# A decoder block on one core: weight buffers moved within 512 bytes, and a few aligned matmuls put ahead of others

## The chip, the cores and the metric

The kernel runs on 1 core of one Trainium2 chip. The metric is device time in microseconds (us), the median of several runs; less is better. TensorE (PE in the profile) does the matmuls, and its weight loads stand under PEld. VectorE is DVE, ScalarE is ACT, GpSimd is POOL; SP issues most DMAs.

## The reference

One decoder layer on 256 tokens of width 1024, float32:

```python
h = rms_norm(x, norm_mix_g);  x = x + hybrid_mixer(h, ...)      # gated convolution and sparse attention, one output projection
h = rms_norm(x, norm_x_g);    x = x + cross_attention(h, mem)   # 4 heads of 256 over 256 memory tokens
h = rms_norm(x, norm_ffn_g);  x = x + swiglu(h, w_in, w_out)    # 1024 -> 2 x 2816 -> 1024
return rms_norm(x, final_norm_g)
```

In `hybrid_mixer` one large projection of `h` gives the convolution's input and gate, 16 queries of 64, three pairs of keys and values (compressed, selected, window; 4 groups) and three sets of gates. With 256 tokens every block of 64 is selected and the window covers everything, so the selected and the window branch are two full causal attentions with their own keys and values.

## The kernel before

**How a float32 product is made.** Activations lie transposed, features on partitions, in eight blocks of 128 features by 256 tokens. A weight chunk is 1024 x 256 and is loaded in two halves of four 128-row blocks (`raw`, L236). `split` (L172) makes a high half (ScalarE copies it rounded to fp32r, L184) and a low half (VectorE subtracts, L186). An activation is parted the same way (`part`, L323). A product is then weight high by activation high, weight high by activation low, weight low by activation high: `rows` (L269, matmuls at L280), 8 matmuls for each of the three in a half, so 48 for a chunk. A matmul has a stationary operand (`lhsT`, 128 x 128, loaded ahead by a weight load) and a moving one (`rhs`, 256 or 512 columns). In most chunks the weight is stationary and the activation moves; with `nat=True` (vs, vw, v) the activation is stationary and the weight moves. A few products (`whole`, L301: k0, kc, vc, q) run in plain fp32 without a split.

**Order of the work.** Memory keys k0 to k3; the convolution's input u0 to u7; kc, vc and queries; ks, kw, vs, vw (keys and values of both branches); gates ga and gc and memory values v, in between which the eight pairs of heads go through `scores`, `weights`, `turned` (transposes, L816) and `output` (L822); pw (convolution's output projection), wo, cross-attention (xq, `cross_scores`, `cross_output`, xo), feed-forward f0 to f21 (L1101), its output fo (L1141), the final norm. The framework's planner orders instructions by priority, but `in_line()` and `behind()` fix the order of most matmuls. The matmuls of xq and xo are only partly fixed.

**A pair's scores** (`scores`, L749): the keys of a group are `kdh` and `kdl`, both branches side by side. For each head a query block of the later 128 tokens meets all 256 keys of both branches (512 moving columns, L761), and one of the first 128 tokens meets 128 keys of both (256 columns, L769). TensorE's order is later half of head 0, first half of heads 0 and 1, later half of head 1. VectorE adds the bias and finds the minimum, first the first halves of both heads (L774), then the later ones (L780); ScalarE takes the exponentials (L795), first halves first. The first halves' PSUM bank, tag `s0`, has one buffer, and the next `turned("b...")` takes it.

**Feed-forward** (L1101 to L1123): for each chunk the high weights meet both parts of the activation in one product of 512 columns (L1113: two outputs of 8 blocks each), then the low weights meet the high part, 256 columns (L1111, 2 x 8). The activation lies in one tile, blocks 0 to 6 as `g`, block 7 as `g8`.

**Where the operands lie.** A tile keeps its place within a partition; a pool gives its tags room in the order of first use. The long slots L0 to L6, L9, LL, L10, L14, L12, L11, L13 come first. The first starts at a multiple of 512 bytes; each is 8,192 bytes except LL (16,896 = 33 x 512) and L14 (8,448 = 16.5 x 512, for `kdl`). So L12, L11 and L13 begin 256 bytes past a multiple of 512 and the others on one. Behind them stands `gap` (L399, 80 elements, 320 bytes), so the five high buffers (`whi`) and the five low ones (`wlo`) begin at 64 modulo 512; each is 4,096 bytes, so all five do. What follows (two small tiles, `vt`, `pr`, `sg`, then `w`, which holds the feed-forward's low halves and the other chunks' raw weights) begins at 128 or, for every second `vt`, at 384. Three halves are placed apart by `set_apart` (L195): k3_0, xq1_0 and xo0_0 have their high half at 256 and their low half at 448.

Below, the **offset** of an operand is its first byte modulo 512, and the **difference** is moving offset minus stationary offset, modulo 256. All rows and blocks within a tile are multiples of 512 apart except where the columns of a block of 256 begin in its second 128, which is 512 bytes on, so a tile has one offset.

Of the kernel before, what the change touches and what calls it, by code (L numbers as in the profile page):

```python
# [10 lines left out]
F32R = mybir.dt.float32r  # L11
# [4 lines left out]
P = 128  # L16
D = 1024
S = 256
# [80 lines left out]
def tile_hybrid_block(  # L99
# [26 lines left out]
    def longs(names, slots, dt=F32R):  # L126
        return [long(n, i, dt=dt) for n, i in zip(names, slots)]
# [6 lines left out]
    def small(name, shape, dt=F32, tag=None, bufs=1):  # L134
        return sb.tile(shape, dt, tag=tag or name, name=name, bufs=bufs)
# [35 lines left out]

    def split(w, shape, name):  # L172
        if name in apart:
            hi = apart[name]()[:, 64:].rearrange("p (k c) -> p k c", k=shape[1])
        else:
            hi = small(f"{name}h", shape, F32R, tag="whi", bufs=5)
        if name in apart:
            lo = aparts[name]().rearrange("p (k c) -> p k c", k=shape[1])
        else:
            lo = small(f"{name}l", shape, F32R, **places[1 - into_ffn(name)])  # L180

        n = 2 if name == "k1_0" else shape[1]
        with behind(*first.get(name, ())):
            copies = [nc.scalar.activation(hi[:, at:at + n], w[:, at:at + n], AF.Copy) for at in range(0, shape[1], n)]  # L184
            for at in range(0, shape[1], n):
                low = nc.vector.tensor_tensor(out=lo[:, at:at + n], in0=w[:, at:at + n], in1=f(hi[:, at:at + n]), op=ALU.subtract)  # L186
        splits[name] = copies[-1], low
        return hi, lo
# [1 line left out]

    first, splits, apart = {}, {}, {}

    aparts = {}

    def set_apart(name, tag, low=None):  # L195

        pair = []

        def hi():
            pair.append(sb.tile([P, 1024 + 64 if low else 2 * 1024 + 112], F32R, tag=tag, name=f"{name}h"))  # L200
            return pair[0][:, 0:1024 + 64]

        def lo():
            if low:
                return sb.tile([P, 1024 + 112], F32R, tag=low, name=f"{name}l")[:, 112:]
            return pair[0][:, 1024 + 112:]

        apart[name], aparts[name] = hi, lo

    set_apart("k3_0", "L14", "L10")  # L210
    set_apart("xq1_0", "LL")
    set_apart("xo0_0", "LL")

# [19 lines left out]
    def into_ffn(name):  # L233
        return name[0] == "f" and name[1] != "o"
# [143 lines left out]
        nc.tensor.matmul(warm, lhsT=ones, rhs=ones, start=True, stop=True)  # L378


    memh, meml, hh, hl, kxh, kxl = longs(("memh", "meml", "hh", "hl", "kxh", "kxl"), range(6))
    mem, h = (memh, meml), (hh, hl)
    mem_t, hf = longs(("mem_t", "hf"), (6, 9), F32)
    _, xt_t, sq = twin("xtsq", F32)
    w = held["k0"] = long("k0w", 10, (P, NB, 256))
# [10 lines left out]
        ahead(name, slot)  # L396
    roots(0)

    small("gap", [P, 80])  # L399

    def kx(j):
        ps = gemm(f"k{j}", mem) if j else whole("k0", mem_t)
# [4 lines left out]
    for i in range(2):  # L407
        hs = slice(4 * i, 4 * i + 4)
        part(memh[:, hs], meml[:, hs], mem_t[:, hs])
    kx(1)  # L410
    for i in range(2):
        hs = slice(4 * i, 4 * i + 4)
        nc.scalar.activation(sq[:, hs], xt_t[:, hs], AF.Square)
# [65 lines left out]
    def convolve(n_v, n_g, *marks):  # L479
# [7 lines left out]
                next(on_g, None)  # L487
        tc.cur_priority = here

    for j in range(NB):  # L490
        ps = gemm(f"u{j}", h)
        sg = small(f"sg{j}", [P, S], tag="sg", bufs=3)
        act = nc.scalar.activation(sg, ps[:, 1], AF.Sigmoid)
        vec = nc.vector.tensor_tensor(out=vt[j][:, PAD:], in0=ps[:, 0], in1=sg, op=ALU.mult)
        convolve((0, 4, 6, 6, 8, 8, 10, 12)[j], (0, 2, 3, 3, 4, 4, 4, 4)[j], act, vec)
# [250 lines left out]
    def heads_of(hp):  # L746
        return 2 * hp, 2 * hp + 1

    def scores(hp):  # L749

        g = hp // 2
        nbp = bias_of(hp)
        s0 = aux(f"s0_{hp}", [P, 2, 2, P], "s0", 1)
        p0 = small(f"p0_{hp}", [P, 2, 2, P], tag="p0", bufs=2)
        s1s, p1 = [], []

        def later_half(hd):
            s1 = aux(f"s1_{hd}", [P, 2, S], "s", 2)
            with in_line():
                for i, t in enumerate((kdh, kdl)):  # L760
                    mm = nc.tensor.matmul(s1, lhsT=qh(hd, 1), rhs=t[:, g].rearrange("p b t -> p (b t)"), start=i == 0, stop=i == 1)  # L761
            last[:] = [mm]
            s1s.append(s1)

        later_half(2 * hp)
        for k, hd in enumerate(heads_of(hp)):
            with in_line():
                for i, t in enumerate((kdh, kdl)):
                    mm = nc.tensor.matmul(s0[:, k], lhsT=qh(hd, 0), rhs=t[:, g, :, 0:P], start=i == 0, stop=i == 1)  # L769
        last[:] = [mm]  # L770
        later_half(2 * hp + 1)
        for k, hd in enumerate(heads_of(hp)):
            for br in range(2):
                red = nc.vector.tensor_tensor_reduce(out=p0[:, k, br], in0=s0[:, k, br], in1=nbp[:, k, P:S], scale=1.0, scalar=3e38,  # L774
                                                     op0=ALU.add, op1=ALU.min, accum_out=mins[:, hd, 0, br:br + 1])
        for k, hd in enumerate(heads_of(hp)):
            p1.append(small(f"p1_{hd}", [P, 2, S], tag="pr", bufs=4))
            for br in range(2):
                with behind(red):
                    low = nc.vector.tensor_tensor_reduce(out=p1[k][:, br], in0=s1s[k][:, br], in1=nbp[:, k], scale=1.0, scalar=3e38,  # L780
                                                   op0=ALU.add, op1=ALU.min, accum_out=mins[:, hd, 1, br:br + 1])
        mins_of.append(low)
        if hp == 1:
            first["gc2_1"] = red,
        return p0, p1

    def weights(hp, p0, p1, *late):

        exp = []
        for qb in range(2):  # L790
            for k, hd in enumerate(heads_of(hp)):
                for br in range(2):
                    t = p1[k][:, br] if qb else p0[:, k, br]
                    with behind(*late) if qb else ExitStack():
                        exp.append(nc.scalar.activation(t, t, AF.Exp, scale=-1.0, bias=mins[:, hd, qb, br:br + 1],  # L795
                                                        accum_out=sums[:, hd, qb, br:br + 1]))
        sc = sums[:, 2 * hp:2 * hp + 2].rearrange("p h t b -> p (h t b)")
        nc.vector.scalar_tensor_tensor(out=sc, in0=sc, scalar=1e-30, in1=igd[:, 2 * hp:2 * hp + 2].rearrange("p h t b -> p (h t b)"),
                                       op0=ALU.max, op1=ALU.mult)
        nc.vector.reciprocal(sc, sc)  # L800
        for k, hd in enumerate(heads_of(hp)):
            for br in range(2):
                nc.vector.tensor_scalar(out=p1[k][:, br], in0=p1[k][:, br], scalar1=sums[:, hd, 1, br:br + 1],
                                        scalar2=None, op0=ALU.mult)
                norm = nc.vector.tensor_scalar(out=p0[:, k, br], in0=p0[:, k, br], scalar1=sums[:, hd, 0, br:br + 1],
                                               scalar2=None, op0=ALU.mult)
        return exp[-1], norm
# [149 lines left out]
    def residual(products, xin, gain, name, slots):  # L957

        xo = long(f"x_{name}", slots[0])
        if len(slots) == 1:  # L960
            t = sb.tile([P, 2 * NB * S + 128], F32R, tag="LL", name=f"g_{name}")
            g = t[:, 16:16 + 14 * S].rearrange("p (c k s) -> p c k s", c=2, k=NB - 1)
            g8 = t[:, 80 + 14 * S:80 + 16 * S].rearrange("p (c s) -> p c s", c=2)
            gh, gl = ([g[:, c, k] if k < NB - 1 else g8[:, c] for k in range(NB)] for c in range(2))
        else:
            gh, gl = longs((f"gh_{name}", f"gl_{name}"), slots[1:])
            xg_ = gh, gl
            gh, gl = ([t[:, k] for k in range(NB)] for t in xg_)
# [87 lines left out]
    def later_half(names, x):  # L1056
# [3 lines left out]
        for n, ps in zip(names, pss):  # L1060
# [5 lines left out]
            if n == names[2]:  # L1066
# [14 lines left out]

    rf = small("rf", [P, S], tag="vw", bufs=4)
    nc.scalar.activation(rf, spread(rnorm(acc2, "3"), "3"), AF.Copy)
    uh, ul = ([long(f"u{c}{i}", n, (P, 6 * S + 16), F32R)[:, 16:].rearrange("p (k s) -> p k s", k=6) for i, n in enumerate(ss)]
              for c, ss in (("h", (4, 2, 1, 12)), ("l", (5, 3, 6, 13))))
    def residual_first():

# [13 lines left out]
    for j in range(NF):  # L1101
        hs = chunk(f"f{j}")
        ab = small(f"ab{j}", [P, 2, S], tag="pr", bufs=4)
        pss = [bank(f"ps_f{j}_{b}") if j % 2 == 0 else aux(f"ps_f{j}_{b}", [P, 2, S], "s", 2) for b in range(2)]
        for part_ in range(2):
            for b, ps in enumerate(pss):
                cs = slice(b * P, b * P + P)
                for kb in range(NB):
                    w = hs[kb // 4][part_][:, kb % 4, cs]
                    if part_:  # L1110
                        nc.tensor.matmul(ps[:, 1], lhsT=w, rhs=fg(kb)[:, 0], start=False, stop=kb == NB - 1)  # L1111
                    else:
                        nc.tensor.matmul(ps, lhsT=w, rhs=fg(kb), start=kb == 0, stop=False)  # L1113
        for b, ps in enumerate(pss):
# [187 lines left out]
```

## Time and profile before

| | us |
|---|---|
| median of 3 runs (550.94 to 551.54) | 551.5 |
| the profiled execution | 551.26 |
| its span, first to last instruction | 549.2 |
| VectorE busy in the span | 417.9 |
| ScalarE busy | 360.4 |
| GpSimd busy | 140.0 |

The span is one execution seen by the profiler; 2.06 us of the execution's own time lie outside it. Engines' busy times overlap. In lists of instructions the form of a line is start, length, engine, source line, operation, output<-inputs, shapes and count; a length reaches from the first start to the last end, and the matmuls are pipelined, so the time of one in a row of them is the difference between starts, not its own length. Buffer numbers are left out of names, so that `k_0h` is the first high half of any of k1 to k3. Transfers bring 512 KB per half chunk, and the f chunks land 3.7 us (median) after their issue.

### The profile page before, as it was taken

What the parts mean: (1) busy time and instruction counts of PE and PEld (TensorE: products, weight loads), DVE (VectorE), ACT (ScalarE), POOL (GpSimd) and SP (SyncE); (2) the same over time, 40 slices, a digit from 0 to 9 for tenths busy, and PEclk for the clock granted to TensorE, in tenths of its full rate; (3) what the DMA queues carried; (4) which work ended last, traced back from release to release, by engine and by line L of the source; (5) the groups of instructions that cost most, each with busy time, mean ns of one, the idle gap of its engine ahead of it and who ended that gap; (6) DMA issues with size and microseconds to landing.
All of it is one profiled execution on the core that took longest, in us unless ns stands there. A gap on an engine that the chain in (4) does not pass through costs nothing.

```text
span 549.2 us, 10209 instructions
## 1 busy us (share of the span) xinstructions
PE 541.3 (99%) x3886; PEld 501.3 (91%) x3886; DVE 417.9 (76%) x781; ACT 360.4 (66%) x681; POOL 140.0 (25%) x125
## 2 busy tenths in 40 slices
PE   8999999999999999999999999999999999999995
PEld 7999998899999999889999999988888888888884
DVE  3888977999998998894868675559878787965531
ACT  4677667679956899689547674477565656463431
POOL 0005999999995001000004100310000000000001
PEclk9999999999999999999999999999999999999999
DMA  8939714456366445334556640466565555177611
GB/s 303 416 125 341 291 25 132 130 170 238 124 214 191 153 144 177 106 116 155 185 198 203 226 150 1 158 226 215 194 204 178 203 175 175 38 237 255 197 40 76
DMA packets 29297, 97.30 MB, mean 177 GB/s; under 512 B 3136, under 2 KB 5440, under 8 KB 28992
## 3 DMA queue, kind: packets, MB, share of 16 engines
q1 hardware_dynamic: 28816, 95.86, 52.3%
q10 hardware_dynamic: 432, 0.79, 0.4%
q8 instruction: 30, 0.49, 0.4%
q14 instruction: 19, 0.16, 0.1%
HBM read 95.39 MB, written 1.25 MB: 176 GB/s over the span
## 4 chain that ended last, share of the span: by engine, by line
PE 94%; DMA 2%; issue 1%; DVE 1%; ACT 1%; SPq 0%; POOLq 0%; POOL 0%; DVEq 0%
PE ps_f L1113 15%; PE fo L1141 10%; PE ps_u L280 8%; PE ps_f L1111 7%; PE ps_q L310 5%; PE ps_ga L280 4%; PE ps_v L280 4%; PE ps_gc L280 4%; PE ps_pw L280 4%; PE ps_xq L280 4%; PE ps_k L280 3%; PE ps_xo L280 3%; PE ps_wo L280 2%; PE ps_xo L1073 2%; PE s L761 1%
## 5 line engine op out<-in xcount | busy, mean ns | idle before, releaser
L466 POOL TENSOR_TENSOR yt<-yt,vw 128x512 f32<-128x512 f32 x61 | 97.0, 1592 | 51.0 <-ACT vw L464 47.4
L464 ACT ACTIVATE vw<-vt,ppt 128x256 f32<-128x256 f32 x102 | 44.3, 498 | 11.4 <-POOL yt L466 11.3
L1113 PE MATMUL ps_f<-g,f_0h 128*128 128x512 f32 x176 | 47.8, 394 | 0.1
L1113 PE MATMUL ps_f<-g,f_1h 128*128 128x512 f32 x176 | 47.6, 391 | 0.0
L1183 POOL TENSOR_SCALAR x<-x,rr 128x512 f32<-128x512 f32 x1 | 0.7, 699 | 176.4 <-DVE rr L1153 176.4
L450 DVE SCALAR_TENSOR_TENSOR yp<-vt,ppt,yp 128x256 f32<-128x256 f32 x108 | 44.1, 480 | 0.2
L186 DVE TENSOR_TENSOR f_0l<-f,f_0h 128x1024 fp32r<-128x1024 f32 x22 | 26.9, 1223 | 19.6 <-PE ps_f L1111 19.6
L1113 PEld LDWEIGHTS ps_f<-g,f_1h 128*128 128x128 f32 x176 | 32.7, 188 | 6.9
L184 ACT ACTIVATE f_1h<-f 128x1024 fp32r<-128x1024 f32 x22 | 23.3, 1060 | 23.2 <-PE ps_f L1113 20.0
L1113 PEld LDWEIGHTS ps_f<-g,f_0h 128*128 128x128 f32 x176 | 31.5, 189 | 5.6 <-DVE ab L1116 0.3
L795 ACT ACTIVATE p<-p,mins 128x128 f32<-128x128 f32 (+1 forms) x64 | 28.3, 445 | 6.7 <-DVE mins L774 6.6
L310 PE MATMUL ps_q<-hf,q 128*128 128x256 f32 x128 | 28.5, 381 | 0.0
L1111 PE MATMUL ps_f<-g,f_0l 128*128 128x256 f32 x176 | 28.1, 281 | 0.0
L1111 PE MATMUL ps_f<-g,f_1l 128*128 128x256 f32 x176 | 28.0, 281 | 0.0
L186 DVE TENSOR_TENSOR f_1l<-f,f_1h 128x1024 fp32r<-128x1024 f32 x22 | 26.8, 1218 | 0.6 <-ACT f_1h L184 0.6
L1111 PEld LDWEIGHTS ps_f<-g,f_0l 128*128 128x128 f32 x176 | 25.5, 188 | 1.8
L310 PEld LDWEIGHTS ps_q<-hf,q 128*128 128x128 f32 x128 | 24.1, 190 | 3.3
L184 ACT ACTIVATE f_0h<-f 128x1024 fp32r<-128x1024 f32 x22 | 23.0, 1046 | 1.8 <-DMA f<-in_wst_dram 1.8
L1111 PEld LDWEIGHTS ps_f<-g,f_1l 128*128 128x128 f32 x176 | 23.9, 189 | 0.0
L1115 ACT ACTIVATE ab<-ps_f 128x256 f32<-128x256 f32 x44 | 16.4, 376 | 6.8 <-PE ps_f L1111 6.8
L981 POOL COPY acc<-s_wo 128x256 f32<-128x256 f32 x1 | 1.1, 1122 | 72.1 <-ACT s_wo L974 72.1
L324 ACT ACTIVATE uh<-sl 128x256 fp32r<-128x256 f32 x22 | 9.2, 418 | 14.3 <-DVE sl L1120 14.3
(550 smaller groups left out, 1555.1 us busy)
## 6 DMA issues: line engine op xcount, KB each, us to landing
f<-in_wst_dram SPq DMA_DIRECT2D x44, 512.0 KB, 3.7
fo<-in_wfo_dram SPq DMA_DIRECT2D x20, 512.0 KB, 4.0
u<-in_wst_dram SPq DMA_DIRECT2D x14, 512.0 KB, 5.7
q<-in_wst_dram SPq DMA_DIRECT2D x8, 512.0 KB, 5.3
ga<-in_wst_dram SPq DMA_DIRECT2D x8, 512.0 KB, 3.7
gc<-in_wst_dram SPq DMA_DIRECT2D x8, 512.0 KB, 3.7
v<-in_wst_dram SPq DMA_DIRECT2D x8, 512.0 KB, 4.3
pw<-in_wst_dram SPq DMA_DIRECT2D x8, 512.0 KB, 5.0
```

Of the source, the lines that this page charges most:

```text
L184: copies = [nc.scalar.activation(hi[:, at:at + n], w[:, at:at + n], AF.Copy) for at in range(0, shape[1], n)]
L186: low = nc.vector.tensor_tensor(out=lo[:, at:at + n], in0=w[:, at:at + n], in1=f(hi[:, at:at + n]), op=ALU.subtract)
L280: mm = nc.tensor.matmul(ps[:, b], lhsT=lhsT, rhs=rhs, start=row + b + kb == 0, stop=kb == NB - 1 and row == 2 and b == 1)
L310: mm = nc.tensor.matmul(ps[:, b], lhsT=w[:, k, cs], rhs=x[:, kb], start=kb + b == 0, stop=kb == NB - 1 and b == 1)
L450: nc.vector.scalar_tensor_tensor(out=out[:, i] if t == ts[-1] else acc[i], in0=v, scalar=w, in1=acc[i], op0=ALU.mult, op1=ALU.add)
L464: nc.scalar.activation(pr[:, i], v, AF.Identity, scale=w, bias=col(PP_DB, j + i) if t == 0 else 0.0)
L466: nc.gpsimd.tensor_tensor(out=y, in0=y, in1=pr, op=ALU.add)
L795: exp.append(nc.scalar.activation(t, t, AF.Exp, scale=-1.0, bias=mins[:, hd, qb, br:br + 1], accum_out=sums[:, hd, qb, br:br + 1]))
L1111: nc.tensor.matmul(ps[:, 1], lhsT=w, rhs=fg(kb)[:, 0], start=False, stop=kb == NB - 1)
L1113: nc.tensor.matmul(ps, lhsT=w, rhs=fg(kb), start=kb == 0, stop=False)
L1115: nc.scalar.activation(ab[:, b], ps[:, 0], AF.Copy)
L1141: nc.tensor.matmul(accs[c][tb], lhsT=t, rhs=w[:, k], start=False, stop=kb == NF - 1 and t is tl)
```

## The change

No matmul, load or arithmetic is added or left out. Operands move, and some instructions change places.

- `gap` shrinks from 80 to 48 elements, so all `whi` and `wlo` buffers begin at 448 instead of 64; `vt` moves to 0 and 256, `pr` to 0; a new `gap2` of 32 elements ahead of `sg` keeps `sg` and `w` where they were.
- `set_apart` places only a high half, at the start of a long slot; the low half goes into the ordinary low ring. k3_0 (offset 0 now), xq1_0 and xo0_0 (0) stay apart, ks_0 (256, slot L11) and k1_0 (0, slot 2) are new. `hh` is allocated after k1 in slot 2.
- The parts of the cross-queries shift with `vt`, from 320 and 64 to 192 and 448.
- A pair's scores are ordered head by head, later half then first half, so that the last two products are those of 256 columns. VectorE's reductions and ScalarE's exponentials go head by head as well.
- In the feed-forward `g` moves from 64 to 192 and `g8` from 320 to 384; the low half begins with block 7 of both outputs, then blocks 0 to 6. Its result `uh`, `ul` moves by 128 bytes, as the output's weights do.

What this makes of the differences:

| products | before | after |
|---|---|---|
| weight stationary (k, u, ks, kw, ga, gc, pw, wo, xq, xo) | 192 | 64 |
| weight moving (vs, vw, v) | 64 | 192 |
| high half of k3_0, xq1_0, xo0_0 | 0 | 0 |
| high half of k1_0, ks_0 | 192 | 0 |
| low half of k3_0, xq1_0, xo0_0 | 64 | 64 |
| pairs' scores; cross outputs; fo | 0 | 0 |
| cross-scores | 192 | 64 |
| f, high weights, blocks 0 to 6 / block 7 | 0 / 0 | 0 / 192 |
| f, low weights, blocks 0 to 6 / block 7 | 192 / 192 | 64 / 0 |

```diff
     def split(w, shape, name):
         if name in apart:
-            hi = apart[name]()[:, 64:].rearrange("p (k c) -> p k c", k=shape[1])
+            hi = apart[name]().rearrange("p (k c) -> p k c", k=shape[1])
         else:
             hi = small(f"{name}h", shape, F32R, tag="whi", bufs=5)
-        if name in apart:
-            lo = aparts[name]().rearrange("p (k c) -> p k c", k=shape[1])
-        else:
-            lo = small(f"{name}l", shape, F32R, **places[1 - into_ffn(name)])
+        lo = small(f"{name}l", shape, F32R, **places[1 - into_ffn(name)])
...
+    def set_apart(name, tag):
+        apart[name] = lambda: sb.tile([P, 1024], F32R, tag=tag, name=f"{name}h")
+
+    set_apart("k3_0", "L14")
+    set_apart("ks_0", "L11")
     set_apart("xq1_0", "LL")
     set_apart("xo0_0", "LL")
...
+    early = long("k1_0h", 2, (P, 1024), F32R)
+    apart["k1_0"] = lambda: early
...
-    small("gap", [P, 80])
+    small("gap", [P, 48])
...
+    hh = long("hh", 2, dt=F32R)
+    h = hh, hl
...
+    small("gap2", [P, 32])
...
         later_half(2 * hp)
+        first_half(0)
         later_half(2 * hp + 1)
+        first_half(1)
+        low = ()
         for k, hd in enumerate(heads_of(hp)):
             p1.append(small(f"p1_{hd}", [P, 2, S], tag="pr", bufs=4))
+            for br in range(2):
+                with behind(*low):
+                    red = nc.vector.tensor_tensor_reduce(out=p0[:, k, br], in0=s0[:, k, br], in1=nbp[:, k, P:S], scale=1.0, scalar=3e38,
+                                                         op0=ALU.add, op1=ALU.min, accum_out=mins[:, hd, 0, br:br + 1])
...
-        for qb in range(2):
-            for k, hd in enumerate(heads_of(hp)):
+        for k, hd in enumerate(heads_of(hp)):
+            for qb in range(2):
...
-            g = t[:, 16:16 + 14 * S].rearrange("p (c k s) -> p c k s", c=2, k=NB - 1)
-            g8 = t[:, 80 + 14 * S:80 + 16 * S].rearrange("p (c s) -> p c s", c=2)
+            g = t[:, 48:48 + 14 * S].rearrange("p (c k s) -> p c k s", c=2, k=NB - 1)
+            g8 = t[:, 96 + 14 * S:96 + 16 * S].rearrange("p (c s) -> p c s", c=2)
...
-    uh, ul = ([long(f"u{c}{i}", n, (P, 6 * S + 16), F32R)[:, 16:].rearrange("p (k s) -> p k s", k=6) for i, n in enumerate(ss)]
+    uh, ul = ([long(f"u{c}{i}", n, (P, 6 * S + 48), F32R)[:, 48:].rearrange("p (k s) -> p k s", k=6) for i, n in enumerate(ss)]
...
-        for part_ in range(2):
+        for part_, kbs in ((0, range(NB)), (1, (NB - 1,)), (1, range(NB - 1))):
             for b, ps in enumerate(pss):
                 cs = slice(b * P, b * P + P)
-                for kb in range(NB):
+                for kb in kbs:
```

More of the change, by code (lines that the diff above doesn't have):

```diff
@@ L191, in tile_hybrid_block @@
     first, splits, apart = {}, {}, {}
[L193 to L210, printed above, removed]
+    def set_apart(name, tag):
+        apart[name] = lambda: sb.tile([P, 1024], F32R, tag=tag, name=f"{name}h")
+    set_apart("k3_0", "L14")
+    set_apart("ks_0", "L11")
     set_apart("xq1_0", "LL")
@@ L378, in tile_hybrid_block @@
         nc.tensor.matmul(warm, lhsT=ones, rhs=ones, start=True, stop=True)
-    memh, meml, hh, hl, kxh, kxl = longs(("memh", "meml", "hh", "hl", "kxh", "kxl"), range(6))
-    mem, h = (memh, meml), (hh, hl)
+    memh, meml, kxh, kxl = longs(("memh", "meml", "kxh", "kxl"), (0, 1, 4, 5))
+    mem = memh, meml
+    early = long("k1_0h", 2, (P, 1024), F32R)
+    apart["k1_0"] = lambda: early
+    hl = long("hl", 3, dt=F32R)
     mem_t, hf = longs(("mem_t", "hf"), (6, 9), F32)
@@ L763, in later_half, with first_half @@
             s1s.append(s1)
-        later_half(2 * hp)
-        for k, hd in enumerate(heads_of(hp)):
+        def first_half(k):
             with in_line():
                 for i, t in enumerate((kdh, kdl)):
-                    mm = nc.tensor.matmul(s0[:, k], lhsT=qh(hd, 0), rhs=t[:, g, :, 0:P], start=i == 0, stop=i == 1)
-        last[:] = [mm]
+                    mm = nc.tensor.matmul(s0[:, k], lhsT=qh(2 * hp + k, 0), rhs=t[:, g, :, 0:P], start=i == 0, stop=i == 1)
+            last[:] = [mm]
+        later_half(2 * hp)
+        first_half(0)
         later_half(2 * hp + 1)
[L772 to L775, printed above, removed]
+        first_half(1)
+        low = ()
         for k, hd in enumerate(heads_of(hp)):
             p1.append(small(f"p1_{hd}", [P, 2, S], tag="pr", bufs=4))
+            for br in range(2):
+                with behind(*low):
+                    red = nc.vector.tensor_tensor_reduce(out=p0[:, k, br], in0=s0[:, k, br], in1=nbp[:, k, P:S], scale=1.0, scalar=3e38,
+                                                         op0=ALU.add, op1=ALU.min, accum_out=mins[:, hd, 0, br:br + 1])
             for br in range(2):
@@ L781, in scores @@
                                                    op0=ALU.add, op1=ALU.min, accum_out=mins[:, hd, 1, br:br + 1])
-        mins_of.append(low)
+            low = low,
+        mins_of.append(low[0])
         if hp == 1:
@@ L789, in weights @@
         exp = []
-        for qb in range(2):
-            for k, hd in enumerate(heads_of(hp)):
+        for k, hd in enumerate(heads_of(hp)):
+            for qb in range(2):
                 for br in range(2):
@@ L1104, in tile_hybrid_block @@
         pss = [bank(f"ps_f{j}_{b}") if j % 2 == 0 else aux(f"ps_f{j}_{b}", [P, 2, S], "s", 2) for b in range(2)]
-        for part_ in range(2):
+        for part_, kbs in ((0, range(NB)), (1, (NB - 1,)), (1, range(NB - 1))):
             for b, ps in enumerate(pss):
                 cs = slice(b * P, b * P + P)
-                for kb in range(NB):
+                for kb in kbs:
                     w = hs[kb // 4][part_][:, kb % 4, cs]
                     if part_:
-                        nc.tensor.matmul(ps[:, 1], lhsT=w, rhs=fg(kb)[:, 0], start=False, stop=kb == NB - 1)
+                        nc.tensor.matmul(ps[:, 1], lhsT=w, rhs=fg(kb)[:, 0], start=False, stop=kb == NB - 2)
                     else:
```

## The prediction

> **What bounds the kernel now.** I read the head of the page first: the span, TensorE's busy time, its clock.
>
> ```profile
> span 549.2 us, 10209 instructions
> PE 541.3 (99%) x3886; PEld 501.3 (91%) x3886; DVE 417.9 (76%) x781; ACT 360.4 (66%) x681; POOL 140.0 (25%) x125
> PEclk9999999999999999999999999999999999999999
> ```
>
> TensorE is busy for all but 7.9 us at the full clock, so only a change in the time of its 3886 matmuls can move the end by much. The change removes and adds none. What can differ is the step, the time from one matmul's start to the next. Next came the chain in order of time (start, length, what, count); its length over its count is the step of a row without a break.
>
> ```profile
> 13.16 5.65 PE ps_k L280 x48
> ...
> 31.94 42.84 PE ps_u L280 x378
> ...
> 121.98 5.65 PE ps_ks L280 x48
> ...
> 138.95 5.65 PE ps_vw L280 x48
> ...
> 168.60 5.66 PE ps_ga L280 x48
> 174.26 5.65 PE ps_gc L280 x48
> ...
> 181.31 3.77 PE ps_gc L280 x32
> ...
> 189.61 4.72 PE ps_gc L280 x40
> ...
> 256.15 21.97 PE ps_pw L280 x192
> ...
> 344.39 8.48 PE ps_xo L1073 x72
> 352.87 5.65 PE ps_xo L280 x48
> ...
> 389.30 3.65 PE ps_f L1113 x16
> 392.95 1.89 PE ps_f L1111 x16
> ...
> 484.84 55.80 PE fo L1141 x246
> ```
>
> All L280, L1073 and L1111 rows are the same shape, 128x128 stationary and 256 moving columns. Yet 42.84/378 is 113.3 ns and 5.65/48 is 117.7 (117.8 over many). u and ks even have equal offsets (moving 0, stationary 64). So one and the same pair of offsets runs at a **short** (113.3) or a **long** (117.8) step, and keeps it over dozens of matmuls: something survives from matmul to matmul, which I call the phase. The third step is in the timeline of TensorE around the second half of k, where k3_0's high half lies at 256 and its low half at 448 (start, length, engine, line; the difference of starts over 8 is the step).
>
> ```profile
> 26.51 1.12 PE L280 MATMUL ps_k<-meml,k_0h 128*128 128x256 f32 x8
> 27.47 1.07 PE L280 MATMUL ps_k<-memh,k_0l 128*128 128x256 f32 x8
> 28.38 1.07 PE L280 MATMUL ps_k<-memh,k_1h 128*128 128x256 f32 x8
> ```
>
> At difference 0 (moving offset minus stationary, modulo 256) the step is 0.96/8 = 120 ns, the **aligned** step; the first eight at difference 64 behind it take 0.91, so 113.3. The same view, later, at the end of the cross outputs (difference 0) and the scores behind them (difference 192):
>
> ```profile
> 330.22 0.64 PE L1038 MATMUL xo_ps<-pxl,vxh 128*128 128x256 f32 x4
> 330.70 0.64 PE L1012 MATMUL xs<-kxh,xqh 128*128 128x256 f32 x4
> 331.17 0.64 PE L1012 MATMUL xs<-kxl,xqh 128*128 128x256 f32 x4
> ```
>
> 0.48/4 = 120 again, then 0.47/4 = 117.5: behind an aligned stretch, 192 goes long where 64 went short. That is the core of the forecast: an aligned stretch sets the phase, and the difference that follows picks the step.
>
> **The change part by part.** Its gain is 4.5 ns for each matmul that goes from the long to the short step, its price 2.2 ns for each long one that becomes aligned (6.7 where it was short). Everything is counted from the profiled execution: 549.2 us of span and 2.06 outside, 551.26, against a median of 551.5.
>
> *k1.* The first 16 go to offset 0, the other 32 to difference 64: 16 x 120 + 32 x 113.3 = 5.55 against 5.65, -0.11. k2's first 24 start behind a short fp32 break; 0, bounds -0.11 to +0.11.
>
> *ks, kw, vs, vw.* Four groups of 48, of which the chain shows the first and last, have the long step: 22.6 us. Afterwards ks_0's high half is aligned (16 at 120) and 176 follow at 113.3: 21.9, so -0.76. vs and vw swap operands and go from 64 to 192; k3's rows show the short step surviving such a crossing (k_0l to k_1h, 64 to 192).
>
> *Gates behind scores.* ga3 and gc0 (96), 32 of gc1 and 40 of gc2 follow a pair's scores and have the long step: 168 matmuls, 19.80 us. Now a pair ends with two aligned 256-column products and the gates stand at difference 64: 168 x 113.3 = 19.04, -0.76. The scores themselves keep their products; 0, bounds +-0.2.
>
> *v behind scores.* It goes to 192, which the cross-score rows put at the long step behind aligned work. It has that now too. 0.
>
> ```profile
> 216.15 1.10 PE L280 MATMUL ps_v<-v_1h,meml 128*128 128x256 f32 x8
> 217.09 0.40 PE L761 MATMUL s<-kdh,qt 128*128 128x512 f32 x1
> ...
> 218.51 1.10 PE L280 MATMUL ps_v<-v_1l,memh 128*128 128x256 f32 x8
> 219.45 1.10 PE L280 MATMUL ps_v<-v_0h,memh 128*128 128x256 f32 x8
> ```
>
> *Restarts.* A stretch that starts behind fp32 work falls into one step or the other. The first row here is such a stretch, at difference 64: 0.94/8, long. Starts at 192 behind the same kind of transpose are mostly short, and so is pw, 21.97/192 = 114.4 with its start. The change swaps the two differences: v's restarts (100 long matmuls) may gain 0.45, the gates' (168 short, ga0 to ga2 among them) may lose 0.76, pw and wo (336) 1.5, xq and what lies between its exchanges -0.3 to +0.7. I take 0, as it is now, since no row shows a start of 64 behind the long fp32 output that precedes pw; all ends stay in the range.
>
> *xo.* Behind the last cross output (aligned) 72 + 48 matmuls run at the long step at 192. They go to 64: 120 x 4.5 = -0.54.
>
> *Feed-forward.* A chunk in the steady part takes 3.65 + 1.89. The low half would be 2 x 120 + 14 x 113.3 = 1.83 instead of 1.89, -0.06. The high half's wide products take 228.1 each against 55.80/246 = 226.8 in the output; if they inherit the better phase, another -0.02 at most, but two of 16 now stand at 192, which no wide row shows: bounds -0.02 to +0.02. I take half, -0.075 a chunk, and 20 of 22 chunks (the first are broken up): -1.5. The output's differences stay 0.
>
> *What else moves.* The second head's two first-half reductions now stand behind the first head's two later-half ones on DVE's queue, and that bank is what the next pt_b needs.
>
> ```profile
> 211.66 0.42 DVE L780 CUSTOM_DVE_ANT_0 p<-s,nb 128x256 f32<-128x256 f32 x1
> 213.86 0.64 PE L816 MATMUL pt_b<-cpt,p 128*128 128x128 f32 x4
> ```
>
> Here first-half reductions end before 211.66, pt_b starts at 213.86, 2.2 us later; two reductions cost 0.84. Cover holds, unless a 1.2 us split gets between; without it TensorE waits a few tenths at each of seven pairs, at most 2 us. The exponentials are the same eight in another order, used a period later: 0. k1_0 and ks_0 leave the ring of five high buffers; k3_0, xq1_0 and xo0_0 bring their low halves into the ring of five low ones. No load is added or moved on SP's or POOL's queue; low halves may be written later by one buffer's turn, at most 24 matmuls or 2.7 us, and TensorE is 99% busy, so I take 0.
>
> Sum: -0.11 - 0.76 - 0.76 - 0.54 - 1.5 = -3.7; 551.26 - 3.7 = **547.6 us**.
>
> The Trainium skill speaks against all of it. Its page "SBUF — State Buffer", section "A bandwidth-pool intuition that's wrong (but worth ruling out)", gives TensorE a second, independent read port for weight loads, and "TensorE: Matmul & The Clock Gate", section "Back-to-back issue gap", makes the step depend on the columns alone (109 ns for 256, by its formula). By these the sum is 0. The trace disagrees: 113.3, 117.7 and 120 for one shape at the full clock.
>
> **The rivals.** *Offsets are not the cause* (the change doesn't do what it says): then the phase comes with what runs around the matmuls and the time stays 551.3. For it: u and ks share their offsets. Against it: all aligned stretches quoted step 120, and no other does. This is the rival that the two rules above give. *Two are too few*: k3's and the cross outputs' aligned stretches are 16 and 24 long, the feed-forward's and the scores' only 2, behind wide ones. Then -1.5 and -0.76 go: 549.8. *Restarts turn*: pw and wo start long, +1.5, a little more from xq: 549.2. *On the other side*: difference 64 does not hold the short step. Quoted rows show it for 8 matmuls, and v has the long one there. Its place is the u loop: if its 378 fall to 117.8 within a chunk, so do k3, ga, pw, wo, xq, some 1000 short ones now, +4.5, while the five gains are gone: about 555.8. Even with the five gains kept it ends slower once some 820 of them turn (820 x 4.5 = 3.7). Better than the forecast by more than a microsecond: v's restarts gain, wides too.
>
> **How the numbers follow.** Forecast with its bounds (546.0 to 548.6) 0.49; two too few 0.16; restarts turn 0.15; offsets not the cause 0.10; other side 0.07; better still 0.03. The range takes the first three and leaves out 0.20: 546.0 to 550.5. About 0.2%, 1.1 us, is what a measurement here tells from no change: faster (under 550.4) 0.80, the first three and the last less 0.03 for the far end of the second; within 0.2% 0.13, that and the offsets' case; slower 0.07.
>
> **What would show it.** In the changed trace, by the differences of starts: k1's first 16 at 120 and the rest at 113.3; ks likewise, and kw, vs, vw 5.44 each; gc behind scores 113.3; u still 42.8 for 378; pw and wo as now; L1073 8.16 for 72; a chunk's L1111 group 1.83 and its L1113 group 3.63 to 3.65. An L1111 group still at 1.89 makes the second rival right, a pw of 22.6 the third, a u of 44.5 the fourth. A wait of TensorE on DVE or ACT at pt_b, or on a split at L186, would break the assumption that nothing else counts. The forecast is wrong altogether if the steps are not set where operands lie.

## The result, and the profile after

The changed kernel takes **555.88 us** (median of 4 runs, 555.58 to 556.23) against 551.22 for the kernel before in the same session: a ratio of 1.0086, 95% interval 1.0069 to 1.0104. It is slower by 4.7 us; 547.6 was forecast. The profiled execution took 556.06, its span is 554.0 against 549.2.

From the head of the page:

```profile
span 554.0 us, 10209 instructions
PE 544.4 (98%) x3886; PEld 503.2 (91%) x3886; DVE 418.9 (76%) x781; ACT 360.0 (65%) x681; POOL 139.9 (25%) x125
```

TensorE is busy 3.1 us longer with the same 3886 matmuls, and idle 9.6 us instead of 7.9. The chain in order of time (start, length, what, count) shows where; L264 is L280 of before, L1068 L1073, L1108 L1113, L1106 L1111.

```profile
13.09 5.54 PE ps_k L264 x48
...
32.02 44.52 PE ps_u L264 x378
...
123.75 5.53 PE ps_ks L264 x48
129.28 5.44 PE ps_kw L264 x48
134.72 5.66 PE ps_vs L264 x48
...
170.45 5.65 PE ps_ga L264 x48
...
258.60 21.96 PE ps_pw L264 x192
...
348.70 6.02 PE ps_xo L1068 x53
...
437.97 3.70 PE ps_f L1108 x16
441.67 1.89 PE ps_f L1106 x16
```

k1, ks and kw came as forecast, to 0.02 us (5.54, 5.53 and 5.44 for 48), and L1068 runs at 6.02/53 = 113.6. But u, which the forecast left at 42.84, takes 44.52, vs kept its long step, the gates behind scores (ga3 here) too, and a feed-forward chunk takes 3.70 + 1.89 instead of 3.65 + 1.89. The steps of each group, added up in the two traces:

| group | forecast, us | measured, us |
|---|---|---|
| k1, k2, k3 | -0.11 | +0.13 |
| u | 0 | +1.70 |
| ks, kw, vs, vw | -0.76 | -0.34 |
| gates behind scores | -0.76 | 0 |
| gates at restarts (ga0 to ga2, the ends of gc1 and gc2, gc3) | 0 | +0.6 |
| v, its wait at pt_b left out | 0 | -0.5 |
| wait at pt_b | 0 | +0.9 |
| wo3 and xq, 0.4 of it waits | 0 | +1.0 |
| xo, all 192 products | -0.54 | -0.44 |
| feed-forward, wide and narrow | -1.5 | +0.5 |
| x's transposes into fo and fo itself, with the wait ahead of f0's last products | 0 | +1.3 |

The table adds up to 4.9; the difference of the spans is 4.8. The last row is mostly one wait, in TensorE's timeline:

```profile
369.31 1.66 PE L1108 MATMUL ps_f<-g,f_1h 128*128 128x512 f32 x6 [0.93 <-DVE g L973]
```

The -0.54 for xo was meant for the 72 products of L1068 and the 48 behind them; these gained 0.53, and the products of xo ahead of them lost 0.09.

### The profile page after: what moved, and what is told of

It reads as the page before. It is cut to its first block, busy times and chain, and to the rows that moved or that the text cites. A ratio compares the mean times of both kernels' runs of the same rounds, so it can differ in the third digit from the quotient of the medians.

```text
span 554.0 us, 10209 instructions
## 1 busy us (share of the span) xinstructions
PE 544.4 (98%) x3886; PEld 503.2 (91%) x3886; DVE 418.9 (76%) x781; ACT 360.0 (65%) x681; POOL 139.9 (25%) x125
## 4 chain that ended last, share of the span: by engine, by line
PE 93%; DMA 2%; DVE 2%; issue 1%; ACT 1%; SPq 0%; POOLq 0%; POOL 0%; ACTq 0%; DVEq 0%
PE ps_f L1108 14%; PE fo L1136 10%; PE ps_u L264 8%; PE ps_f L1106 8%; PE ps_q L294 5%; PE ps_ga L264 4%; PE ps_gc L264 4%; PE ps_xq L264 4%; PE ps_pw L264 4%; PE ps_v L264 3%; PE ps_wo L264 3%; PE ps_k L264 3%; PE ps_xo L264 2%; PE pt_a L811 1%; PE ps_kc L294 1%; PE o L835 1%
## 5 line engine op out<-in xcount | busy, mean ns | idle before, releaser
L455 POOL TENSOR_TENSOR yt<-yt,vw 128x512 f32<-128x512 f32 x61 | 94.4, 1549 | 53.6 <-DMA vcw<-in_wst_dram 46.2
L1108 PE MATMUL ps_f<-g,f_1h 128*128 128x512 f32 x176 | 48.1, 394 | 0.9 <-DVE g L973 0.9
L1108 PE MATMUL ps_f<-g,f_0h 128*128 128x512 f32 x176 | 48.1, 395 | 0.0
L1108 PEld LDWEIGHTS ps_f<-g,f_1h 128*128 128x128 f32 x176 | 32.7, 188 | 8.4 <-DVE g L973 1.2
L1108 PEld LDWEIGHTS ps_f<-g,f_0h 128*128 128x128 f32 x176 | 31.4, 188 | 5.9
L1106 PE MATMUL ps_f<-g,f_1l 128*128 128x256 f32 x176 | 31.6, 280 | 0.0
L1106 PEld LDWEIGHTS ps_f<-g,f_1l 128*128 128x128 f32 x176 | 26.9, 188 | 1.8
L1106 PE MATMUL ps_f<-g,f_0l 128*128 128x256 f32 x176 | 28.4, 281 | 0.0
L1106 PEld LDWEIGHTS ps_f<-g,f_0l 128*128 128x128 f32 x176 | 24.1, 188 | 0.1
```

The lines of the kernel that those rows point to most:

```text
L455: nc.gpsimd.tensor_tensor(out=y, in0=y, in1=pr, op=ALU.add)
```

## The experiments

**A kernel of matmuls alone (e4, e5).** Wide products have 512 moving columns, narrow ones 256; "at 64" means at difference 64. The kernel has rows of products at chosen differences, each behind a row that sets a known step. In its names `X` is the activation, and `zero`, `quarter`, `half` and `threeq` are weight tiles that give it the difference 0, 64, 128 and 192; `psf` is plain fp32. Where the tile's name stands behind the arrow first, the weight moves.

> A kernel of matmuls alone on a 128 x 2048 activation, nothing of the layer is computed: rows of products of 256 and 512 columns at chosen differences, each behind a row that first sets the short step (8 fp32 products, 24 aligned, 16 at 64) or the long one (8 fp32, 24 aligned, 16 at 192). Theory: behind fp32 work a row at 64 or 192 falls into 113.3 or 117.8 by where the fp32 row left off; an aligned row of n out of the long step leads to 113.3 at 64 only when n is long enough (8 to 24, not 2 or 4), and out of the short step any n does; 64 to 192 with the weight stationary keeps the step; with the operands swapped it goes to 117.8; wide products at difference 0 take 226.7 in both, and at 192 some ns more. Rival: the step at a difference is fixed by that difference and the last aligned stretch, whatever came ahead of the stretch: then 2 aligned products are as good as 24.

Timeline of TensorE in e4: a row at 192 with the long step, two aligned products, a row at 64, and the fp32 row behind it.

```profile
207.13 2.05 PE L45 MATMUL ps<-X,threeq 128*128 128x256 f32 x16
209.01 0.40 PE L45 MATMUL ps<-X,zero 128*128 128x256 f32 x2
209.25 2.88 PE L45 MATMUL ps<-X,quarter 128*128 128x256 f32 x24
211.97 0.81 PE L45 MATMUL psf<-XF 128*128 128x256 f32 x3
```

(211.97 - 209.25)/24 = 113.3: out of a narrow row at 192, two aligned products are enough, as the rival had it, and 4, 8, 16 and 24 give the same. Straight behind fp32 products rows at 64 and 192 ran long in four starts of four, behind transposes in three of four. Now a short row at 64 that is followed by a row with the operands swapped, its weights at 192:

```profile
327.86 1.98 PE L45 MATMUL ps<-X,quarter 128*128 128x256 f32 x16
329.68 3.93 PE L45 MATMUL ps<-quarter,X 128*128 128x256 f32 x32
333.45 1.81 PE L45 MATMUL ps<-X,quarter 128*128 128x256 f32 x14
```

(333.45 - 329.68)/32 = 117.8: this crossing, that of kw to vs, loses the short step at once. With the weight stationary on both sides of 64 to 192 it holds (113.4 over 32), and it also holds when the operands swap and the difference stays 64 (113.4 over 32). And the scores as the change orders them (two wide, two narrow, twice; one row of eight here), behind a short row and ahead of one at 64:

```profile
380.73 1.56 PE L45 MATMUL ps<-X,zero 128*128 128x512 f32 x8
382.12 2.99 PE L45 MATMUL ps<-X,quarter 128*128 128x256 f32 x24
384.95 1.24 PE L45 MATMUL psf<-XF 128*128 128x256 f32 x5
```

(384.95 - 382.12)/24 = 117.9: behind wide products two aligned ones set nothing. Their own steps are 113 to 122, never a steady 120.

> A second kernel of matmuls alone, with rows that the first did not have. Theory (an aligned row sets the phase only once it has come to its own 120 ns; how soon that is hangs on what it is entered from): out of a row that is long at 64, 16 aligned products show the uneven steps of k3_0 (117 to 124) and leave the next row long, while 48 may settle; behind fp32 work 4 to 8 aligned products are enough; behind wide products 2 are not (steps 113 to 115) and 4 to 8 are, so four wide and then four narrow ones let a row at 64 run at 113.3; a row at 192 behind them runs at 117.8. Rival (the count alone decides): what n does behind wide products it does behind narrow and fp32 ones too, and 16 out of a long row at 64 are enough.

Timeline of TensorE in e5, three rows that are long at 64, behind each 16, 24 and 48 aligned products, then 64 again:

```profile
48.05 2.08 PE L45 MATMUL ps<-X,zero 128*128 128x256 f32 x16
49.97 2.99 PE L45 MATMUL ps<-X,quarter 128*128 128x256 f32 x24
52.80 3.62 PE L45 MATMUL psf<-XF 128*128 128x256 f32 x16
...
59.08 3.04 PE L45 MATMUL ps<-X,zero 128*128 128x256 f32 x24
61.95 2.88 PE L45 MATMUL ps<-X,quarter 128*128 128x256 f32 x24
64.67 1.67 PE L45 MATMUL psf<-XF 128*128 128x256 f32 x7
...
70.95 5.92 PE L45 MATMUL ps<-X,zero 128*128 128x256 f32 x48
76.72 3.00 PE L45 MATMUL ps<-X,quarter 128*128 128x256 f32 x24
79.55 0.81 PE L45 MATMUL psf<-XF 128*128 128x256 f32 x3
```

The rows at 64 take 117.9, 113.3 and 117.9: 16 fail, 24 succeed, 48 fail. The steps inside tell why: the 24 stand at an even 120 from the sixth on, the 16 and the 48 run round a cycle of five, 117 118 121 120 124, whose mean is 120 too, and never leave it. So it isn't the count (2, 4 and 8 out of such a row fail too). In these rows a stretch that has settled at an even 120 leaves the next one short at 64, and one that hasn't leaves it long; of two products alone that can't be read off. Behind fp32 products 2, 4 and 8 weren't enough and 16 were; the theory's "4 to 8" was wrong there. Behind sixteen wide products three were enough:

```profile
403.56 4.17 PE L45 MATMUL ps<-X,zero 128*128 128x512 f32 x19
407.57 1.64 PE L45 MATMUL ps<-X,quarter 128*128 128x256 f32 x13
409.04 4.17 PE L45 MATMUL ps<-X,zero 128*128 128x512 f32 x19
```

Sixteen wide ones and three narrow stand in the first row; the thirteen at 64 take (409.04 - 407.57)/13 = 113.1. Behind four wide and four narrow ones a row at 192 was short and one at 64 long, which is the reverse of what the forecast took for a law.

**u: another half placed apart (e3).**

```diff
-    set_apart("k3_0", "L14")
+    set_apart("k2_1", "L14")
```

> The kernel after with another half placed apart: k2_1's high half (its 16 products start behind two fp32 products) lies at 0 in slot L14 instead of k3_0's (which is entered out of a row of long steps). Theory (an aligned stretch settles the phase when it starts behind fp32 work, and difference 64 then holds the short step as long as nothing breaks the row): k2's last 8, k3 and u stand at 113.3, u 42.8 us instead of 44.5; time 554.0, 1.9 us under after. Rival (difference 64 does not hold the short step over hundreds of products): k3 starts short and u falls back to 117.8 within a chunk or two; time 555.6.

In the changed kernel's own timeline k3_0's aligned products come out of a long row at 64 (k2 restarts long behind its fp32 break):

```profile
25.46 1.13 PE L264 MATMUL ps_k<-memh,k_0h 128*128 128x256 f32 x8
26.43 1.12 PE L264 MATMUL ps_k<-meml,k_0h 128*128 128x256 f32 x8
27.38 1.10 PE L264 MATMUL ps_k<-memh,k_0l 128*128 128x256 f32 x8
28.33 1.10 PE L264 MATMUL ps_k<-memh,k_1h 128*128 128x256 f32 x8
```

0.97 and 0.95 for eight, single steps of 117, 118, 121, 120, 124 round and round, and behind them 117.9. With the stretch behind the fp32 products instead, the chain of e3 reads

```profile
23.09 7.36 PE ps_k L264 x64
...
32.03 42.84 PE ps_u L264 x378
```

All 378 are short again. Time 553.52 against 551.57, ratio 1.0035 (1.0022 to 1.0048): 2.4 us under the changed kernel's median, 2.7 if each is taken against before in its own session, where 1.9 were expected; in its profile the wait at f0 is 0.5 shorter and that ahead of wo3 0.4. Difference 64 does hold the short step over hundreds; the row was entered in the wrong phase.

**The scores' order (e1).** The order of the scores, of VectorE's reductions and of ScalarE's exponentials as before; all offsets as after.

```diff
         later_half(2 * hp)
-        first_half(0)
+        for k, hd in enumerate(heads_of(hp)):
+            ...
         later_half(2 * hp + 1)
-        first_half(1)
```

> The kernel after with the scores of a pair, VectorE's reductions and ScalarE's exponentials in the order of before; all operands stay where the change put them. Theory (the order costs a wait at the first v pair and the two narrow products set nothing): TensorE's wait of 0.8 us on mins at pt_b goes, the gates behind a pair's scores stay at 117.8, v behind scores goes back to 117.8 (+0.3 us); time 555.2, 0.3 to 0.9 us under after. Rival (the two narrow aligned products are what keeps v short and part of the gates): the gates and v lose 0.5 us or more and the time is 555.9 or above.

The changed kernel's timelines of VectorE and TensorE at the first pair that v follows:

```profile
213.46 1.22 DVE L183 TENSOR_TENSOR v_0l<-v,v_0h 128x1024 fp32r<-128x1024 f32 x1
214.60 0.28 DVE L770 CUSTOM_DVE_ANT_0 p<-s,nb 128x128 f32<-128x128 f32 x1
...
215.92 0.29 DVE L770 CUSTOM_DVE_ANT_0 p<-s,nb 128x128 f32<-128x128 f32 x1
```

```profile
216.36 0.63 PE L811 MATMUL pt_b<-cpt,p 128*128 128x128 f32 x4 [0.79 <-DVE mins L770]
```

A 1.22 us split stands ahead of the reductions, and the second head's first halves come behind the first head's later ones; the last one ends at 216.21 and TensorE has waited 0.79. In e1 that wait is gone (v0's 48 steps add up to 0.96 less), the gates behind scores are as long as before, and v keeps what it had gained: that gain comes from its restarts at 192, not from the order. Time 554.33 against 551.57, ratio 1.0047 (1.0032 to 1.0062). The span is 1.7 us shorter; the rest of that is the waits ahead of wo3 and at f0 (0.46 and 0.93 in the changed kernel's profile, none and 0.47 in this one), whose length differs from profile to profile.

**The feed-forward put back (e2).**

```diff
-            g8 = t[:, 96 + 14 * S:96 + 16 * S]...
+            g8 = t[:, 112 + 14 * S:112 + 16 * S]...
-        for part_, kbs in ((0, range(NB)), (1, (NB - 1,)), (1, range(NB - 1))):
+        for part_ in range(2):
```

> The kernel after with the feed-forward alone put back: g8 lies as many bytes from the high weights as g, so all wide products have difference 0, all narrow ones 64, in the order of before. Theory (the block at difference 192 lengthens the wide products and the two aligned narrow ones set nothing): the wide group of 16 goes back to 3.65 us from 3.70, the narrow group stays at 1.88 to 1.90; 22 chunks give 1.0 us, time 554.9. Rival (with 64 in place of 192 the narrow ones behind sixteen aligned wide ones turn short): narrow group 1.82, another 1.4 us, 553.5. Second rival (the wide ones are long for the phase in which they are entered, not for block 7): 555.9.

A chunk in its chain:

```profile
387.40 3.69 PE ps_f L1108 x16
391.09 1.89 PE ps_f L1106 x16
```

The wide products stay long (3.69, not 3.65) though none stands at 192 any more, so the second rival is right: what they cost is the narrow row ahead. Behind narrow ones that are long at 64 the first ten wide steps are 241 237 234 236 224 230 236 229 232 230 (f4); in the kernel before, behind long ones at 192, five are uneven (233 236 228 233 231) and the rest 227. e4 shows the same, 3.69 behind 64 and 3.65 behind 192. Time 555.48 against 551.57, ratio 1.0072 (1.0055 to 1.0089), which can't be told from the changed kernel's 1.0086.

**Four aligned products in place of two (e6).** The wide ones all aligned; from f2 on the low halves of blocks 6 and 7 lie in slots 0 and 9, free by then, at 192 like the activation, and come first. With k2_1 apart and the old order of scores.

```diff
+        if kick:
+            lok = sb.tile([P, 48 + 512], F32R, tag=f"L{9 * (int(name[1:-2]) % 2)}", ...)[:, 48:]...
-        for part_, kbs in ((0, range(NB)), (1, (NB - 1,)), (1, range(NB - 1))):
+        for part_, kbs in ... if j < 2 else ((0, range(NB)), (1, (6, 7)), (1, range(6))):
```

> The kernel after with k2_1 placed apart in place of k3_0, the scores' order of before, and another feed-forward: all wide products aligned; from the third chunk on the low halves of blocks 6 and 7 lie in the long slots 0 and 9 at 192, so that the narrow products begin with four aligned ones and twelve at 64 follow. Theory (behind sixteen wide ones three or four aligned products bring the aligned step back to 120 and the next row at 64 is short; the wide ones behind a short row settle as in before): a narrow group of 16 takes 1.83 us in place of 1.89 (4 at 118, 12 at 113.3), a wide group 3.65 in place of 3.70, so 20 chunks give 2.1 us; with 1.9 of k2_1 and 0.9 of the wait at pt_b that is 4.9 under after, 551.0. Rival (the kernel's operands lie in more places than those of the matmuls alone, and the four aligned ones set nothing): narrow groups 1.89, wide ones 3.69, 552.9.

```profile
389.21 3.65 PE ps_f L1108 x16
392.86 1.83 PE ps_f L1106 x16
```

Both numbers of the theory stand in its chain, in every chunk from f4 to f20: narrow steps 113 119 120 121 in the one shown, then twelve at 113.3. Time 550.91 against 552.12, ratio 0.9976 (0.9967 to 0.9986).

**Four wide, then four narrow (e7, e8).**

```diff
         later_half(2 * hp)
+        later_half(2 * hp + 1)
         for k, hd in enumerate(heads_of(hp)):
             ...
-        later_half(2 * hp + 1)
```

> The kernel before with one edit: a pair's scores go on TensorE as both later halves, then both first halves; all operands stay. Theory (behind four wide and four narrow aligned products a row at 192 is short): the gates behind a pair's scores, ga3, gc0, 32 of gc1 and 40 of gc2, go from 117.8 to 113.3, 0.76 us; v at 64 stays long; no wait is added at pt_b, since the first halves end only a quarter of a microsecond later and still come first on VectorE; time 550.6. Rival (the phase behind scores does not hang on their order): 551.4, nothing changes.

The gates in the chain of e8, against the four rows of before that stand in the prediction:

```profile
168.54 5.44 PE ps_ga L280 x48
173.99 5.44 PE ps_gc L280 x48
...
180.82 3.63 PE ps_gc L280 x32
...
188.99 4.54 PE ps_gc L280 x40
```

All 168 are short, 19.05 instead of 19.80, at 192 and with no operand moved. But the first halves end later, one step ahead of the first v's pt_b now takes 390 ns instead of 119, a wait that the expectation had ruled out, and TensorE waited 0.50 ahead of wo3 and 0.38 at f0 in that execution: 551.75 against 552.12, ratio 1.000 (0.9989 to 1.0011). The theory's row came, its time can't be told from no change.

> As the kernel with the feed-forward's four aligned products, and two more edits: a pair's scores go as both later halves, then both first halves (four wide, then four narrow aligned products), with VectorE's order of before; and wo3_0's high half is placed apart (behind a break) in place of xq1_0's (entered out of a row). Theory (behind four wide and four narrow aligned products 192 runs short and 64 long, as in the matmuls alone): v behind scores, at 192, goes to 113.3, some 100 products, 0.45 us; the gates at 64 stay at 117.8; wo3 and xq0 ahead of the next break go to 113.3, 0.3 us; time 0.7 us under that kernel. Rival (two times two narrow ones are as good or bad as four): v stays, only wo3 and xq0 gain, 0.3 us.

v0's first 24 products behind scores went to 113.3 after three uneven steps, and a step of 359 ns ahead of pt_b took that back; of all of v, 160 steps are short against 122 in e6. ga3, gc0 and gc1 behind scores stayed long, but the 40 of gc2 did not, against the expectation:

```profile
189.58 4.54 PE ps_gc L269 x40
```

The eight products of scores ahead of them step 233 231 226 227, 113 119 120 121; ahead of ga3 and gc1 the narrow ones step 112 117 118 115. So four wide and four narrow products don't settle by themselves what follows. With wo3_0 apart wo3 and xq0 take 10.99 us, against 11.02 in e6, where wo3 was short already. Time 550.93 (ratio 0.9981, 0.9965 to 0.9998) beside 550.91 of e6: nothing. Its profiled execution, at 553.93 the longest of its ten, also shows what the wait at f0 is. ScalarE's timeline, then TensorE's:

```profile
364.56 1.06 ACT L185 ACTIVATE f_0h<-f 128x1024 fp32r<-128x1024 f32 x1 [3.37 <-DMA f<-in_wst_dram]
...
366.04 0.89 ACT L972 ACTIVATE g<-x,ppt 128x256 fp32r<-128x256 f32 x2
```

```profile
367.34 2.45 PE L1108 MATMUL ps_f<-g,f_1h 128*128 128x512 f32 x6 [2.79 <-DVE g L973]
```

f2's first high half waits for its load, 3.37 us here, on ScalarE's queue ahead of the last residual's g, which f0 needs.

**f2's split behind the residual (e9, e10).** One edit, on e6 and on the kernel before; `mark` is the copy that makes the residual's last g.

```diff
+        first["f2_0"] = mark,
```

> The kernel with k2_1 apart, the scores' order of before and the feed-forward's four aligned products, and one more edit: on ScalarE the high half of f2_0, which waits for its load, comes behind the last square and parts of the cross-attention's residual instead of ahead of them. Theory (TensorE's wait at f0 for DVE's last g is that load, ahead of g on ScalarE's queue): the wait, 0.8 us in that kernel, 0.9 in after and 0.4 to 2.8 in the others, is gone and nothing waits in its place, since f2 is needed some 7 us later; time 550.1, and with it 1.3 us or 0.25% under before. Rival (the load is late for f2 as well, and the wait moves to f1 or f2): 550.9.

> The kernel before with that one edit on ScalarE's queue. Theory: the profiled execution of before shows no wait at f0, so the edit gives nothing there; where another execution's load comes later it saves some tenths; 551.3, at most 0.5 us under before. Rival (before has that wait in most executions and its profile was a lucky one): 550.5.

From the head of e9's page:

```profile
PE 540.3 (99%) x3886; PEld 500.5 (91%) x3886; DVE 424.0 (77%) x801; ACT 356.1 (65%) x681; POOL 139.3 (25%) x125
```

No wait at f0 is left in e9; it takes **550.33 us against 551.82, ratio 0.9971 (0.9962 to 0.998)**, and so beats both kernels. What the edit adds to e6 (0.9976) can't be told from nothing: in e9's profile TensorE waits ahead of wo3, and wo3 and xq take 0.8 more than in e6's. On the kernel before the edit gives 551.31, ratio 0.9991 (0.9981 to 1.0001): 0.5 us, 1.0 at the interval's end and not clear of nothing. So most of e9's 1.5 us is the steps.

## Why the prediction was wrong

*The core, "an aligned stretch sets the phase, and the difference that follows picks the step".* This is the step that failed. It was read from two stretches, one entered out of a short row at 192, one long enough to settle. In the runs the phase is set by an aligned row that has come to an even 120, and whether it comes there hangs on the row ahead: two products are enough out of a row at 192, 16 behind fp32 work, three or four behind sixteen wide ones; out of a long row at 64, 24 did and 16 and even 48 didn't. That cost u 1.7 us where the sum had 0, left the gates behind scores at 0 where it had -0.76, and the feed-forward at +0.5 where it had -1.5. The second half fell too: behind four wide and four narrow products 192 was the short one (e5, e8). Why the offsets modulo 256 matter at all, no run shows.

*k1, ks, kw.* Right to 0.02 us a group. *xo.* Right: 8.17 for the 72 of L1068 against 8.16, and 0.53 gained on the 120; the eight aligned cross outputs ahead, entered out of a long row at 64, came to 120 and 121. *k2, "0, bounds -0.11 to +0.11".* +0.10, inside its bounds by luck: the first 24, which it meant, stayed at 2.91, and the other 24, behind the second fp32 break, went long. It is yet the costliest of all: a long k2 at 64 hands its phase to k3's aligned 16, they stay in the cycle of five, and u pays 1.7 us. The bound was put on k2's own products, not on what they hand on.

*vs, vw.* k3's rows showed a crossing from 64 to 192 with the weight stationary on both sides; vs swaps the operands at that place, and e4 shows that this alone loses the step.

*Gates and feed-forward.* The rival "two are too few" is right in both places (e4, e5), but its 549.8 left out that the feed-forward also loses: moving the narrow row from 192 to 64 costs the wide ones 0.04 of their 0.05 a chunk through the row ahead (e2), not through block 7, where the working put its bound of 0.02.

*Restarts.* Costed at 0 with wide bounds. pw and wo0 to wo2 stayed short, v gained 0.5, the gates lost 0.6, wo3 and xq about 1.0 with 0.4 of waits in it; the sum lies inside the bounds that were kept. Which step a restart takes isn't settled: at 64 pw starts short and most gates start long. For wo3 a wait ahead of it matters. At 64 it began behind a wait in the changed kernel, e3 and e9 (first step 222 to 226 ns) and ran at 117.8; without a wait it ran at 113.3 in e2 and e6, though at 117.8 in e1. At 192 it began behind a wait as well, in before, e8 and e10, and came to 113.3 within five products.

*Cover of pt_b.* The working named the case, "unless a 1.2 us split gets between". It did, once, for 0.79 us. *The low ring, 0.* A wait of 0.9 us appeared at f0; e7 and e9 show that it is a load's lateness behind ScalarE's order, which comes out from 0.4 to 2.8 us long in the profiled executions of seven kernels here and is missing from before's own. One of the seven is e8, with all operands as before (0.38), so the low ring isn't needed for it, and part of the 0.9 may be the luck of one execution.

*The other side.* Its 555.8 is the measured time to 0.1 us and its u is 44.5, but as a mechanism it is wrong: e3 runs all 378 short at 64, and pw, which it had long, stayed short. u, k3, ga0 to ga2, wo3 and xq, which it named, give some 2.9 of its 4.5, entered long and not fallen; pw and wo0 to wo2 give nothing, and k1, ks, kw and xo keep gains of 0.9 that it had gone. Waits and wide products, which it didn't have, fill the gap. The agreement is chance.

By the Trainium skill, "TensorE: Matmul & The Clock Gate", section "Back-to-back issue gap", u would have the same step in the changed kernel and in e3; the traces have 117.8 and 113.3.

## What to carry to other kernels

Where the step of a matmul depends on history, an alignment can't be judged from its own rows: follow the phase from each break to the next, and ask what a row hands on as well as what it costs. Before moving operands through a whole kernel, run the candidate rows alone, entered out of each row that really stands ahead of them; two such runs showed four of the failed terms. A change that promises tenths of a per cent has to keep the queues as they are: two short waits took 1.7 us here.

## What the runs showed of the hardware

- The step of an fp32r product with 256 columns has at least four patterns at one clock (e4, e5, granted 0.999): even 113.3, mean 117.8, even 120, and a cycle of five (117 118 121 120 124) at difference 0 that 48 products don't leave. Two rows at difference 128 step 113 to 124, on the mean 118.3 and 118.7 (e4).
- A wide product at difference 192 steps 236 ns among aligned ones of 227 (e4).
- After the wait of 2.79 us in e7 TensorE resumed at 367.34 and ran at half rate from 367.95 to 371.36 (granted clock 0.50): wide steps of 427, narrow ones of 214 to 217. The view by windows gives the granted clock over wider stretches (after the busy times of five engines):

```profile
360.00:364.00 4.00, 4.00 (x23) 3.24 (x22) 2.22 (x3) 1.06 (x1) 0.00 (x0) 1.00 0.98 345
367.30:370.90 3.60, 3.56 (x13) 3.09 (x14) 1.46 (x2) 2.58 (x4) 0.57 (x1) 0.59 0.03 11
```

The clock goes from 1.00 to 0.59 there, so a wait of under 3 us can cost more than its own length. The Trainium skill ("TensorE: Matmul & The Clock Gate", section "What's actually happening") has half rate after one idle window of about 3.4 us; here an idle time of 2.8 was enough.
